# A gated linear recurrence on one core: dense scores in chunks of 128 tokens with three states each way, in place of scores for halves with one state each way

## The chip, the core and the metric

The kernel runs on one core of one Trainium2 chip. The metric is the device time of one execution in microseconds; three runs of the kernel before gave a median of 1075.76 us (1075.6 to 1076.09). Engines are named as in the profile: PE is TensorE's matmul, PEld its weight load, DVE is VectorE, ACT is ScalarE, POOL is GpSimd, SP is SyncE.

## The reference

Two layers, each with three branches on 512 tokens of width 1024. The change concerns branch A alone, a gated linear recurrence that runs over the tokens forward and backward for each of four heads (key and value width 128):

```python
def step(S, xs):
    qc, kc, vc, lfc = xs
    b = jnp.cumsum(lfc, axis=2)
    diff = b[:, :, :, None, :] - b[:, :, None, :, :]
    decay = jnp.exp(jnp.where(tri[None, None, :, :, None], diff, -jnp.inf))
    scores = jnp.einsum('bhtd,bhtsd,bhsd->bhts', qc, decay, kc)
    o = jnp.einsum('bhts,bhsv->bhtv', scores, vc) + jnp.einsum('bhtd,bhdv->bhtv', qc * jnp.exp(b), S)
    b_end = b[:, :, -1, :]
    S_new = jnp.exp(b_end)[..., None] * S + jnp.einsum(
        'bhsd,bhsv->bhdv', kc * jnp.exp(b_end[:, :, None, :] - b), vc)
    return S_new, o
```

The outputs of the two directions are added, normalised per head (an RMS norm over the 128 values) and multiplied by a SiLU gate. How the tokens are cut into chunks is free, since any cut gives the same sums: a pair of tokens (t, s) needs the product of q, k and of all gates between them.

## The kernel before

Most of the time goes to the projections: `t_block` (L516), `nat_part` (L469) and `parts_of_product` (L1200) run float32r matmuls of 512 or 256 columns in three passes (high parts, low parts of the activations, low parts of the weights) into `pm` PSUM tiles, of which there are three (`ps_main`). The weights come by DMA, are split by ScalarE and VectorE (L266, L267) a step ahead, and are used once.

Everything else is side work, written as Python generators. The main line calls `advance(us)` behind each half block of projections. It adds the time of that half block to a credit and, while the credit is positive, runs the next steps of the first two generators of the list `sides` in turn; a generator yields its own cost in us, or None to wait for the next call. The credit is cut to twice the half block's time, or to zero when the list is empty. `flush` runs generators to their end with no projections between. A scheduler of the compiler then orders each engine's instructions, so that the order in the trace can differ from the one written. Side work puts its PSUM results into `ps` tiles, of which there are five (`ps_side`).

Branch A is `gla(h, ...)`, one generator for each head. Heads run in pairs: `together` takes one step of both heads at a time, so a visit of the side work to PE holds both heads' instructions. There are two pairs in each of two layers, four in all; the second pair of a layer runs beside the branch projections `merge` and, at its end, beside `gate`.

Inside `gla` the scores of one head are built by levels m = 1, 2, 4, ..., 128. At level m a block of m tokens is paired with its neighbour block of m tokens (k of the one, q of the other, in either direction): `compact` (L925) does the levels up to 8 in 32x32 pieces, L950 the levels 16 and 32, L959 the level 64, and L974 the level 128, which pairs the two chunks of 128 tokens in each half of 256. After a level, q (`qd`, both directions) and k (`kd`) are multiplied by the gates of the neighbour block (L983, two products of 128x512 a level), and the block gates `ff` are multiplied in pairs (L986). So after level 128 q and k carry the decay to the border of their half.

The scores lie in `pm`, 128 partitions by four chunks by 256 columns, a tile of the pool `m4` (nineteen buffers of 4 KB a partition): the first copy (L963) writes the 128x128 diagonal blocks, copied predicates (L966) put the small levels into them, and L975 writes the blocks of level 128. Then, one step each: `kt`, four transposes of k (L998) copied to `kts` by L1000; the states `st`, four matmuls (L1005), two for each half of 256 tokens, copied to `sts` by L1009: one state goes from the first half to the second (forward), and one from the second to the first (backward); and the outputs `po`, for each chunk two products with `pm` (L1015) and one of q with the other half's state (L1022). `kts`, `sts`, `q`, `ksum`, `kx` (L914), the value tile `vC` of the attention and several others are tiles of the pool `t2`, seven buffers of 2 KB a partition. The normalisation follows (L1024, L1026, `rstd` at L320 to L331, L1031), then four transposes (L1036) and the product with the gate (L1037).

Of the kernel before, what the change touches and what calls it, by code (L numbers as in the profile page):

```python
# [12 lines left out]
F32 = mybir.dt.float32  # L14
# [7 lines left out]
P = 128  # L22
# [169 lines left out]
def build(nc, tc, cp, wp, sb, pp, dp, x, wpk, brow, gainb, pvec, wsp, trig, amask, imask, out):  # L192
# [397 lines left out]
    for l in range(L):  # L590
# [304 lines left out]
        def gla(h, q, ff, kd, z):  # L895
# [8 lines left out]
            pm = m4((P, 4, 256))  # L904
# [25 lines left out]
            def diag_dst(off, n):  # L930
                return custom(pm, off, ([512, 2], [384, 2], [1, n]))

# [6 lines left out]
            while m < 256:  # L939
# [16 lines left out]
                elif m == 64:  # L956
# [6 lines left out]
                    S.copy(diag_dst(0, P), dg.rearrange("p (a b) t -> p a b t", a=2))  # L963
                    for qu in range(4):
                        pr = slice(32 * qu, 32 * qu + 32)
                        V.copy_predicated(  # L966
                            diag_dst(32 * qu, 32)[pr],
                            im[pr, 4, :].unsqueeze(1).unsqueeze(1).broadcast_to((32, 2, 2, 32)),
                            pc[pr].rearrange("p (a b) t -> p a b t", a=2),
                        )  # L970
                else:
                    l128 = ps_side((P, 4, P))
                    for c in range(4):
                        E.matmul(l128[:, c, :], k_op(P * c, m), q_op(P * (c ^ 1), m), start=True, stop=True)  # L974
                    S.copy(  # L975
                        custom(pm, 128, ([512, 2], [128, 2], [1, P])), l128.rearrange("p (a b) t -> p a b t", a=2)
                    )
# [6 lines left out]
                if m < 128:  # L984
                    ffn = sb.tile([P, 2, ng], F32, name=nm("f2"), tag=f"f2_{h % 2}_{lvl % 2}", bufs=1)
                    V.tensor_tensor(ffn, fv[:, :, :, 0], fv[:, :, :, 1], ALU.mult)  # L986
                    ff = ffn
# [8 lines left out]
            kt = ps_side((P, 4, P))  # L996
            for c in range(4):
                E.transpose(kt[:, c, :], k_op(P * c, m), ident)  # L998
            kts = t2((P, 4, P))
            S.copy(kts, kt)  # L1000
            yield None
            st = ps_side((P, 2, P))
            for hf in range(2):
                for c in range(2):
                    E.matmul(  # L1005
                        st[:, hf, :], kts[:, 2 * hf + c, :], vA[hf][:, c, h * P : (h + 1) * P], start=c == 0, stop=c == 1
                    )
# [531 lines left out]
```

## Time and profile before

| | |
|---|---|
| median of three runs | 1075.76 us |
| the profiled execution | 1076.32 us |
| its span in the profile | 1074.6 us |
| PE busy | 1063.3 us (99%) |
| PEld busy | 900.7 us (84%) |
| DVE busy | 822.7 us (77%) |
| ACT busy | 491.7 us (46%) |
| POOL busy | 106.9 us (10%) |
| TensorE clock granted | full in all 40 slices |

A busy time counts each engine's instructions from their start to their end. For matmuls the end is modelled and lies behind the start of the next one, so durations of matmuls can't be added up; starts can be compared. A group of instructions is named by its line, engine and operation, then by the tiles that it writes and reads (`ps` and `pm` are PSUM tiles, `m` stands for `m4`, `t` for `t2`, `sm` for small columns). In a row of a group the count stands behind x, then busy us and the mean ns of one, then the idle time of that engine just before and what ended it.

### The profile page before, as it was taken

The page shows a single profiled execution, that of the slowest core. Times are in us where ns is not written, and L with a number is a line of the kernel's source. Part 1 is how long each engine was busy: PE and PEld are TensorE (multiplying, and loading weights), DVE is VectorE, ACT ScalarE, POOL GpSimd, SP SyncE. Part 2 cuts the span into 40 slices and gives each one's busy share as a digit, 9 for nine tenths or more (in the row PEclk, how much of TensorE's full clock was granted, in tenths as well). Part 3 has the DMA queues.
Part 4 walks back from the last instruction along what each step waited for, and adds up shares of the span by engine and source line. Part 5 has one row for each costly group of instructions (what it writes and reads, how often), then busy time and mean ns, then how long its engine had stood idle before and what let it go on. Part 6 is the DMA issues. An engine that isn't in the chain of part 4 may idle for free.

```text
span 1074.6 us, 18675 instructions
## 1 busy us (share of the span) xinstructions
PE 1063.3 (99%) x7480; PEld 900.7 (84%) x7480; DVE 822.7 (77%) x1553; ACT 491.7 (46%) x749; POOL 106.9 (10%) x150
## 2 busy tenths in 40 slices
PE   9999999999999999999999999999999999999998
PEld 8888877878788898988778888777877888999886
DVE  6974799897965975578887578998697759675885
ACT  5344665353523553545433366554444246445442
POOL 0220111000000000001112201100000001010020
PEclk9999999999999999999999999999999999999999
DMA  8673454153333464664958445434414235566665
GB/s 309 175 213 110 160 177 150 61 207 106 113 118 88 90 196 119 157 230 103 294 162 235 123 145 190 157 119 129 149 58 136 101 59 113 181 138 170 207 169 141
DMA packets 49736, 162.74 MB, mean 151 GB/s; under 512 B 5745, under 2 KB 10353, under 8 KB 49649
## 3 DMA queue, kind: packets, MB, share of 16 engines
q1 hardware_dynamic: 28656, 100.20, 28.4%
q0 software_dynamic: 19264, 57.16, 21.5%
q10 hardware_dynamic: 1728, 4.20, 1.0%
q8 instruction: 59, 0.97, 0.4%
q14 instruction: 29, 0.23, 0.1%
HBM read 139.51 MB, written 22.02 MB: 150 GB/s over the span
## 4 chain that ended last, share of the span: by engine, by line
PE 91%; DVE 5%; ACT 1%; issue 1%; DMA 1%; POOL 0%; SPq 0%; POOLq 0%; ACTq 0%; DVEq 0%
PE pm L516 48%; PE pm L469 12%; PE ps L1200 10%; PE pm L1200 9%; PE pm L504 2%; PE ps L830 2%; PE ps L925 1%; DMA wr<-in_wpk 1%; PE ps L1015 1%; PE ps L780 1%; PE ps L781 1%; DVE wl L267 1%; PE ps L974 1%; PE ps L1005 1%; PE ps L1080 1%
## 5 line engine op out<-in xcount | busy, mean ns | idle before, releaser
L266 ACT CAST wh<-wr 128x1024 fp32r<-128x1024 f32 x160 | 167.0, 1051 | 226.2 <-PE pm L516 101.9
L267 DVE TENSOR_TENSOR wl<-wr,wh 128x1024 fp32r<-128x1024 f32 x160 | 193.6, 1221 | 70.7 <-PE pm L516 42.3
L516 PE MATMUL pm<-hth,wh 128*128 128x512 f32 x576 | 230.1, 399 | 0.0
L516 PE MATMUL pm<-htl,wh 128*128 128x512 f32 x576 | 225.3, 391 | 0.0
L516 PE MATMUL pm<-hth,wl 128*128 128x512 f32 x576 | 225.0, 391 | 0.0
L516 PEld LDWEIGHTS pm<-hth,wh 128*128 128x128 f32 x576 | 108.3, 188 | 24.0 <-issue 2.9
L516 PEld LDWEIGHTS pm<-hth,wl 128*128 128x128 f32 x576 | 108.2, 188 | 23.0 <-DVE wl L267 0.2
L516 PEld LDWEIGHTS pm<-htl,wh 128*128 128x128 f32 x576 | 108.3, 188 | 21.6 <-issue 1.3
L516 PE MATMUL pm<-m,wh 128*128 128x512 f32 x256 | 90.0, 392 | 0.2 <-ACT m L1150 0.2
L983 DVE TENSOR_TENSOR m<-m,f 128x512 f32<-128x512 f32 x112 | 73.7, 688 | 5.5 <-PE ps L950 3.5
L469 PE MATMUL pm<-wh,hth 128*128 128x512 f32 x192 | 74.6, 398 | 0.7 <-ACT hth L266 0.6
L469 PE MATMUL pm<-wh,htl 128*128 128x512 f32 x192 | 73.5, 392 | 0.2 <-DVE htl L267 0.2
L469 PE MATMUL pm<-wl,hth 128*128 128x512 f32 x192 | 73.2, 392 | 0.0
L267 DVE TENSOR_TENSOR wl<-hold,wh 128x1024 fp32r<-128x1024 f32 x36 | 43.7, 1222 | 20.2 <-PE pm L1200 15.1
L266 ACT CAST wh<-hold 128x1024 fp32r<-128x1024 f32 x36 | 37.7, 1047 | 43.1 <-PE pm L516 19.6
L516 PEld LDWEIGHTS pm<-m,wh 128*128 128x128 f32 x256 | 47.8, 188 | 9.7 <-ACT m L1150 0.4
L516 PE MATMUL pm<-t,wl 128*128 128x512 f32 x128 | 50.3, 393 | 0.0
L516 PE MATMUL pm<-t,wh 128*128 128x512 f32 x128 | 50.0, 391 | 0.0
L469 PEld LDWEIGHTS pm<-wh,hth 128*128 128x128 f32 x192 | 36.0, 188 | 10.3 <-ACT hth L266 1.4
L469 PEld LDWEIGHTS pm<-wh,htl 128*128 128x128 f32 x192 | 36.1, 188 | 7.6 <-DVE htl L267 0.5
L469 PEld LDWEIGHTS pm<-wl,hth 128*128 128x128 f32 x192 | 36.1, 188 | 7.5
L266 ACT CAST m<-m 128x512 fp32r<-128x512 f32 (+1 forms) x30 | 24.4, 821 | 38.4 <-DVE m L1321 22.1
(258 smaller groups left out, 2248.1 us busy)
## 6 DMA issues: line engine op xcount, KB each, us to landing
wr<-in_wpk SPq DMA_DIRECT2D x160, 512.0 KB, 4.2
pd<-m POOLq DMA_DIRECT2D x20, 512.0 KB, 3.8
m<-pd POOLq DMA_DIRECT2D x20, 512.0 KB, 5.2
hold<-in_wpk POOLq DMA_DIRECT2D x18, 512.0 KB, 5.5
hold<-in_wpk SPq DMA_DIRECT2D x12, 512.0 KB, 4.4
wr<-in_wpk POOLq DMA_DIRECT2D x12, 512.0 KB, 7.2
m<-in_x SPq DMA_DIRECT2D x8, 512.0 KB, 7.7
m<-xd POOLq DMA_DIRECT2D x16, 256.0 KB, 7.0
```

Source lines behind the costliest of these rows:

```text
L266: order(S.copy(hi_dst, src))
L267: order(eng.tensor_tensor(lo_dst, src, hi_dst.bitcast(F32), ALU.subtract))
L469: E.matmul(po, a, b[:, o : o + 512], start=first and n == 0, stop=last and n == len(passes) - 1)
L504: E.matmul(po[:, k, :], a, b[:, o : o + 256], start=n == 0, stop=n == 23)
L516: E.matmul(po, s, m, start=n == 0, stop=n == 3 * nk - 1)
L780: E.matmul(sp[:, :nk], qt[qb][:, h, :], ktt[0][:, g, k0 * P : k1 * P], start=True, stop=False)
L781: E.matmul(sp[:, :nk], qt[qb][:, h, :], ktt[1][:, g, k0 * P : k1 * P], start=False, stop=True)
L830: E.matmul(po[64 * g : 64 * g + 64], vC[:, k0 + kb, 64 * g : 64 * g + 64], pt[:, :, 128 * g : 128 * g + 128], start=kb == 0, stop=kb == le ...
L925: E.matmul(cb[p0 : p0 + 32, slot, j // 4, :], kk(32 * j), qq(32 * j), start=True, stop=True, tile_position=(0, p0),)
L974: E.matmul(l128[:, c, :], k_op(P * c, m), q_op(P * (c ^ 1), m), start=True, stop=True)
L983: V.tensor_tensor(v, v, custom(ff, of, ([sd, 2], [2, ng], [0, m])), ALU.mult)
L1200: E.matmul(banks[g][:, r, :], a, b, start=not onto and (r, kt, n) == (0, 0, 0), stop=kt == 3 and n == 2, skip_group_check=onto is not None ...
```

## The change

The levels end at m = 64, so `pm` holds only the four 128x128 diagonal blocks, without gaps, and becomes a tile of `t2`. The level 128 goes, with its matmuls, its copy and its two products on q and k, and with one step of the generator. The part between chunks is done by states at the chunk borders instead: for each direction three chunks of k are transposed and give three states of one chunk each; a scaled addition on VectorE (the state of the chunk before, times the gate of the chunk, plus the chunk's own state) makes running states out of them, two in each direction one behind the other. An output chunk takes one product with its diagonal scores, one with the forward state where there is a chunk before it, and one with the backward state where there is one behind it. `kts` and `sts` exist once for each direction.

```diff
--- before.py
+++ after.py
@@ -1,3 +1,4 @@
+
 
 
 
@@ -901,7 +902,7 @@
             V.tensor_tensor(qd, ff, q.unsqueeze(1).broadcast_to((P, 2, T)), ALU.mult)
             cb = ps_side((P, 4, 4, 32))
             pc = sb.tile([P, 4, 32], F32, name=nm("pc"), tag="pc", bufs=2)
-            pm = m4((P, 4, 256))
+            pm = t2((P, 4, P))
 
             def q_op(t0, m):
                 if m < 32:
@@ -927,16 +928,13 @@
                         start=True, stop=True, tile_position=(0, p0),
                     )
 
-            def diag_dst(off, n):
-                return custom(pm, off, ([512, 2], [384, 2], [1, n]))
-
             m, lvl, nb = 1, 0, T
             kx = k_mix(m)
             yield 2.6
             yield None
             compact(0, lambda t: ksum[:, t : t + 32], lambda t: q[:, t : t + 32])
             V.tensor_copy(pc, cb[:, 0])
-            while m < 256:
+            while m < P:
                 if m <= 8:
                     slot = (lvl + 1) % 4
                     compact(slot, lambda t: kx[:, t : t + 32], lambda t: q_op(t, m))
@@ -953,38 +951,28 @@
                             q_op(32 * jq, m),
                             start=True, stop=True, tile_position=(0, p0),
                         )
-                elif m == 64:
+                else:
                     for j in range(8):
                         p0, f0 = 64 * (j % 2), 64 * ((j ^ 1) % 2)
                         E.matmul(
                             dg[p0 : p0 + 64, j // 2, f0 : f0 + 64], k_op(64 * j, m), q_op(64 * (j ^ 1), m),
                             start=True, stop=True, tile_position=(0, p0),
                         )
-                    S.copy(diag_dst(0, P), dg.rearrange("p (a b) t -> p a b t", a=2))
+                    S.copy(pm, dg)
                     for qu in range(4):
                         pr = slice(32 * qu, 32 * qu + 32)
                         V.copy_predicated(
-                            diag_dst(32 * qu, 32)[pr],
-                            im[pr, 4, :].unsqueeze(1).unsqueeze(1).broadcast_to((32, 2, 2, 32)),
-                            pc[pr].rearrange("p (a b) t -> p a b t", a=2),
+                            pm[pr, :, pr], im[pr, 4, :].unsqueeze(1).broadcast_to((32, 4, 32)), pc[pr]
                         )
-                else:
-                    l128 = ps_side((P, 4, P))
-                    for c in range(4):
-                        E.matmul(l128[:, c, :], k_op(P * c, m), q_op(P * (c ^ 1), m), start=True, stop=True)
-                    S.copy(
-                        custom(pm, 128, ([512, 2], [128, 2], [1, P])), l128.rearrange("p (a b) t -> p a b t", a=2)
-                    )
 
                 ng = nb // 2
                 fv = ff.rearrange("p s (g b) -> p s g b", b=2)
                 for t, of, sd in ((qd, 1, nb - 1), (kd, nb + 1, -nb - 1)):
                     v = custom(t, 0, ([T + m, 2], [2 * m, ng], [1, m]))
                     V.tensor_tensor(v, v, custom(ff, of, ([sd, 2], [2, ng], [0, m])), ALU.mult)
-                if m < 128:
-                    ffn = sb.tile([P, 2, ng], F32, name=nm("f2"), tag=f"f2_{h % 2}_{lvl % 2}", bufs=1)
-                    V.tensor_tensor(ffn, fv[:, :, :, 0], fv[:, :, :, 1], ALU.mult)
-                    ff = ffn
+                ffn = sb.tile([P, 2, ng], F32, name=nm("f2"), tag=f"f2_{h % 2}_{lvl % 2}", bufs=1)
+                V.tensor_tensor(ffn, fv[:, :, :, 0], fv[:, :, :, 1], ALU.mult)
+                ff = ffn
                 m *= 2
                 nb //= 2
                 lvl += 1
@@ -993,33 +981,39 @@
                 yield 2.6
                 yield None
 
-            kt = ps_side((P, 4, P))
-            for c in range(4):
-                E.transpose(kt[:, c, :], k_op(P * c, m), ident)
-            kts = t2((P, 4, P))
-            S.copy(kts, kt)
+
+            def v_of(c):
+                return vA[c // 2][:, c % 2, h * P : (h + 1) * P]
+
+            kts = []
+            for d in range(2):
+                kt = ps_side((P, 3, P))
+                for c in range(3):
+                    E.transpose(kt[:, c, :], kd[:, d, P * (c + d) : P * (c + d + 1)], ident)
+                kts.append(t2((P, 4, P)))
+                S.copy(kts[d][:, 0:3], kt)
             yield None
-            st = ps_side((P, 2, P))
-            for hf in range(2):
-                for c in range(2):
-                    E.matmul(
-                        st[:, hf, :], kts[:, 2 * hf + c, :], vA[hf][:, c, h * P : (h + 1) * P], start=c == 0, stop=c == 1
-                    )
-            sts = t2((P, 2, P))
-            S.copy(sts, st)
+            sts = []
+            for d in range(2):
+                st = ps_side((P, 3, P))
+                for c in range(3):
+                    E.matmul(st[:, c, :], kts[d][:, c, :], v_of(c + d), start=True, stop=True)
+                s3 = t2((P, 4, P))
+                order = (2, 1, 0) if d else (0, 1, 2)
+                S.copy(s3[:, order[0]], st[:, order[0]])
+                for a, b in zip(order, order[1:]):
+                    c = b + d
+                    c = max(a, b)
+                    V.scalar_tensor_tensor(s3[:, b], s3[:, a], ff[:, 1 - d, c : c + 1], st[:, b], ALU.mult, ALU.add)
+                sts.append(s3)
             yield None
             po = ps_side((P, 4, P))
             for t in range(4):
-                hf = t // 2
-                for c in range(2):
-                    E.matmul(
-                        po[:, t, :],
-                        pm[:, 2 * hf + c, (t % 2) * P : (t % 2 + 1) * P],
-                        vA[hf][:, c, h * P : (h + 1) * P],
-                        start=c == 0,
-                        stop=False,
-                    )
-                E.matmul(po[:, t, :], q_op(P * t, m), sts[:, 1 - hf, :], start=False, stop=True)
+                E.matmul(po[:, t, :], pm[:, t, :], v_of(t), start=True, stop=False)
+                if t > 0:
+                    E.matmul(po[:, t, :], qd[:, 1, P * t : P * t + P], sts[0][:, t - 1, :], start=False, stop=t == 3)
+                if t < 3:
+                    E.matmul(po[:, t, :], qd[:, 0, P * t : P * t + P], sts[1][:, t, :], start=False, stop=True)
             y = t2((P, 4, P))
             S.activation(y, po, AF.Square)
             ss = small(4)
```

## Rows read from the trace of the kernel before

**Rows 1.** page, part 1: span; busy us, share and instructions of each engine
```profile
span 1074.6 us, 18675 instructions
PE 1063.3 (99%) x7480; PEld 900.7 (84%) x7480; DVE 822.7 (77%) x1553; ACT 491.7 (46%) x749; POOL 106.9 (10%) x150
```

**Rows 2.** page, part 4: the chain that ended last, by engine
```profile
PE 91%; DVE 5%; ACT 1%; issue 1%; DMA 1%; POOL 0%; SPq 0%; POOLq 0%; ACTq 0%; DVEq 0%
```

**Rows 3.** waits of PE: waiter <- releaser: us in total, times, longest
```profile
PE ps L1036 <- DVE t L1031: 1.5, 2, 0.8
PE ps L1036 <- DVE sm L330: 1.0, 2, 0.6
```

**Rows 4.** PE in order of time, level 128: start us, us, line, count
```profile
327.50 0.39 PE L516 MATMUL pm<-hth,wl 128*128 128x512 f32 x1
327.73 1.95 PE L974 MATMUL ps<-m,m 128*128 128x128 f32 x16
329.43 0.48 PE L516 MATMUL pm<-hth,wh 128*128 128x512 f32 x1
329.75 0.40 PE L516 MATMUL pm<-htl,wh 128*128 128x512 f32 x1
```

**Rows 5.** the same: transposes, states, and outputs with what follows them
```profile
337.70 1.03 PE L998 MATMUL ps<-ident,m 128*128 128x128 f32 x8
338.49 0.48 PE L516 MATMUL pm<-hth,wh 128*128 128x512 f32 x1
...
341.31 1.95 PE L1005 MATMUL ps<-m,t 128*128 128x128 f32 x16
343.01 0.71 PE L516 MATMUL pm<-m,wh 128*128 128x512 f32 x2
...
345.82 0.60 PE L1015 MATMUL ps<-m,m 128*128 128x128 f32 x4
...
351.10 0.48 PE L516 MATMUL pm<-hth,wh 128*128 128x512 f32 x1
```

**Rows 6.** groups by form, PE: shapes, count; busy us, mean ns; idle before
```profile
L1015 PE MATMUL ps<-m,m 128*128 128x128 f32 x128 | 19.5, 275 | 0.0
L974 PE MATMUL ps<-m,m 128*128 128x128 f32 x64 | 7.8, 275 | 0.0
L998 PE MATMUL ps<-ident,m 128*128 128x128 f32 x32 | 4.1, 272 | 0.0
```

**Rows 7.** groups by form, VectorE and ScalarE
```profile
L983 DVE TENSOR_TENSOR m<-m,f 128x512 f32<-128x512 f32 x112 | 73.7, 688 | 5.5 <-PE ps L950 3.5 <-PE ps L959 1.0 <-ACT t L914 0.8
L1069 DVE SCALAR_TENSOR_TENSOR br<-ps,pvc,br 128x128 f32<-128x128 f32 x8 | 2.6, 331 | 0.0
L975 ACT COPY m<-ps 128x512 f32<-128x512 f32 x8 | 4.6, 585 | 5.9 <-PE ps L974 5.9
L1000 ACT COPY t<-ps 128x512 f32<-128x512 f32 x8 | 4.3, 590 | 2.3 <-PE ps L998 2.3
L1009 ACT COPY t<-ps 128x256 f32<-128x256 f32 x8 | 3.0, 370 | 8.3 <-PE ps L1005 8.3
```

**Rows 8.** PE in order of time at the last transposes; idle time and releaser bracketed
```profile
365.11 0.40 PE L1200 MATMUL pm<-m,wh 128*128 128x256 f32 x2
365.88 0.63 PE L1036 MATMUL ps<-ident,t 128*128 128x128 f32 x4 [0.37 <-DVE sm L330]
367.26 0.63 PE L1036 MATMUL ps<-ident,t 128*128 128x128 f32 x4 [0.75 <-DVE t L1031]
367.65 0.36 PE L1200 MATMUL ps<-hth,wh 128*128 128x256 f32 x1
```

**Rows 9.** waits of ScalarE
```profile
ACT t L914 <- PE ps L1036: 3.6, 2, 1.8
```

**Rows 10.** groups by form, weight loads of level 128
```profile
L974 PEld LDWEIGHTS ps<-m,m 128*128 128x128 f32 x64 | 7.8, 192 | 0.3
```

## The prediction

> **What bounds the kernel now.** I read the shares of the engines first: TensorE (PE) is busy for 1063.3 of 1074.6 us, VectorE (DVE) for 77% and ScalarE (ACT) for 46% [rows 1]. A busy PE need not be a bounding one, so the chain that ended last came next: 91% of it runs over PE [rows 2]. Third, the list of what PE waited for. Its longest entries are 1.5 and 1.0 us in the whole span, both ahead of the last transposes of the recurrence (L1036) [rows 3]. So PE sets the time almost everywhere, and the recurrence, though it is "side work" put between the blocks of the projections, is paid for in full: a PE instruction taken out of it shortens the span as long as nothing makes PE wait instead.
>
> The price of one PE instruction is not its duration in the group list (275 ns, whose end is modelled and overlaps the next one [rows 6]) but the spacing of the starts. I took it from the order in time. At the level m = 128 of the second pair of heads in layer 0, sixteen instructions start at 327.73 and the next projection matmul starts at 329.43: 1.70 us. That first matmul behind them then takes 0.32 us to the next start (329.43 to 329.75) instead of 0.23 (327.50 to 327.73), so the visit costs 1.70 + 0.09 = 1.79 us, 0.112 us for each instruction [rows 4]. The same way eight transposes cost 0.79 + 0.09 = 0.88 (0.110 each), sixteen instructions of the states 1.70 + 0.09 = 1.79, and 48 of the outputs 5.28 + 0.09 = 5.37 (0.112 each) [rows 5]. Visits of this kind cost their instructions and hardly any entry fee; each occurs four times (two pairs of heads in each of two layers), with the same gaps.
>
> **The change part by part.** The counts show that a float32 matmul of 128 columns stands as two instructions and a transpose as one: four matmuls by eight heads give x64 at L974, four transposes by eight give x32 at L998, and eight products with the scores give x128 at L1015 [rows 6]. For each pair of heads, on PE:
> - The level m = 128 goes: 2 x 4 matmuls, 16 instructions, -1.79 us.
> - Transposes of k: from 2 x 4 to 2 x 6 (three chunks each way), +4 x 0.110 = +0.44.
> - States: from 2 x 4 matmuls to 2 x 6, +8 instructions x 0.112 = +0.90.
> - Outputs: from 2 x 12 matmuls (eight with scores, four with states) to 2 x 10 (four, and three each way), -8 x 0.112 = -0.90.
>
> Sum -1.35 us a pair, four pairs, -5.4 us. All of it lies on PE, which has no cover to lose.
>
> The other engines. VectorE loses two products of 128x512 a head, 2 x 0.688, and gains four scaled additions of 128x128 out of PSUM; the nearest row is L1069, the same operation on the same shape, 0.331 [rows 7]. That is -1.376 + 1.324, nothing. ScalarE loses copies of 0.585, 0.590 and 0.370 a head; from 512 to 256 columns a copy falls by 0.220, so 384 columns are estimated at 0.48 and 128 at 0.26, two of each, 1.48 against 1.545, nothing again [rows 7]. The copy into `pm` and the four predicated copies keep their element counts: nothing. No DMA is issued, removed or moved, and no queue of SP or POOL is passed. The removed round held one `yield 2.6` a head.
>
> What is new is a chain. Before, the outputs needed only one copy of 256 columns behind the states. Now each direction needs a copy (0.26) and two dependent additions (0.331 each), about 0.92 us; two directions of two heads put 8 x 0.331 = 2.65 us on VectorE between the states and the first output that needs them. The cover is the twelve projection matmuls between the two visits, 343.01 to 345.82, 2.8 us, and the states' own visit (now 24 x 0.112 = 2.7 us), in which the first chains already run [rows 5]. So the first head's chains are covered twice, the second head's by 2.8 against 0.92 plus whatever VectorE has queued ahead; behind a late output PE's in-order queue holds the projections. The trace of before has no such wait; the nearest row is L1036, where VectorE comes late with a similar small chain and PE idles 0.37 and 0.75 us [rows 8], 2.5 us over two visits [rows 3], 1.25 a visit. I bound the new wait by 0 and 2.5 us a pair (one such wait for each head), and take 0: it is nearest to the present outputs, which follow their copies without idle time [rows 5]. A gain here has no source, since there was no wait.
>
> The L1036 wait itself (2.5 us in the two second pairs) I keep. Walking `advance` and `step` with the costs written in the code, the first pair ends one round earlier, the side list then runs empty, its credit is cut to zero, and the second pair starts a round of credit later; its last three rounds fall behind the same projection blocks as before. Its bounds are 0 and twice itself, so -2.5 to +2.5.
>
> Buffers: `pm` moves from the nineteen `m4` to the seven `t2`, and a head has two `kts` and two `sts` where it had one of each. The pool is already full at times: the copy of L914 waits for L1036 for 3.6 us in two waits, although it reads only k, so what it waits for is a buffer [rows 9]. In a first pair, with `vC` and the next head's `q` still alive, two `pm` and four states make eight, so the second head's last state waits for the first head's outputs and PE may see one more chain of 0.92: 0 to 0.9 us in two pairs, 0 to 1.8 in all. I take 0, because PE has projection blocks to put there, and an eviction held up by the pool stops PE only when all three `pm` PSUM banks are full. [...]
>
> The sum: -5.4 us. The profiled execution took 1076.32 us, 1.72 more than its span of 1074.6, so 1070.9 for it; it lies 0.56 above the median of 1075.76, and from the median the forecast is 1070.4 us. A measurement of this kernel can tell about 0.2% (2.15 us) from no change.
>
> **The rivals.**
> - *The wait at L1036 goes too.* If the earlier end of the chains lets the last normalisation run ahead of the sums of the next stage on VectorE, 2.5 us more are gained: 1067.9. For it: VectorE has 2.8 us a pair less in the removed round. Against it: the credits above put the tail where it was.
> - *Half of it comes back.* One wait of 1.25 us a pair at the outputs, 4 x 1.25 = 5.0: -0.4, 1075.4, within 0.2%.
> - *Slower: PE waits for the states' chains.* The place is the first output with a state, in all four pairs; both heads wait 1.25, 2.5 a pair, 10 us in all: +4.6, 1080.3. It decides from (5.4 + 2.15) / 4 = 1.9 us a pair. For it: two dependent additions and a copy more, a full `t2` pool, and VectorE at 77%. Against it: 2.8 us of projections between the visits, and more to be put there.
> - *Weight loads set the pace.* If each instruction cost what its weight load lasts, 0.192 us [rows 10], and the transposes' the 0.11 above, then 16 x 0.192 - 0.44 = 2.63 a pair would go, 10.5 in all: 1065.2. Against it: the sixteen start 0.106 us apart [rows 4], so loads overlap each other. [...]
>
> **How the numbers follow.** Forecast with up to 2.5 us either way (1068.3 to 1073), 0.62; L1036 gone, 0.12; weight loads, 0.04; half back, 0.12; slower, 0.10. Faster by over 0.2% is 0.62 + 0.12 + 0.04 = 0.78, within 0.12, slower 0.10. The range takes in the first, second and fourth case: 1067.0, a little under 1067.9, to 1076.0, a little over 1075.4; it leaves out 0.14.
>
> **What would show it.** PE's instructions fall by 6 a head (-8, +2, +4, -4), 48 in all, from 7480 to 7432. Transposes stand as x48 and states as x96; no 128x512 copy follows a level 128. The spacing in the new visits is 0.11 us. The four additions a head are near 0.33 us, 32 in all. PE's wait list shows no entry of over 1 us at an output line; if it shows the additions as releaser there, the third or second rival holds. The span falls by 5.4 us. I am wrong if the count falls as said and the span does not: then PE's idle time or its gaps have grown, and the line behind the gap names the step.

## The result, and the profile after

The changed kernel takes 1067.13 us (median of four runs, 1066.56 to 1067.98), beside 1075.70 for the kernel before on the same chip (1075.6 to 1076.09): a ratio of 0.992, 95% interval 0.9903 to 0.9937, or 8.6 us less. The forecast was 1070.4, 5.4 us less. The sign was right, but 3.2 us more went than the instructions account for, and the time lies only 0.1 us above the lower end of the range (1067.0). The profiled execution took 1067.56 us with a span of 1065.8; the span fell by 8.8 us, and the ledger below is made against that.

The page of the changed kernel, parts 1 and 4 (span, busy us of each engine, the chain that ended last), which answers to [rows 1, 2]:

```profile
span 1065.8 us, 18593 instructions
PE 1057.0 (99%) x7432; PEld 894.3 (84%) x7432; DVE 822.6 (77%) x1569; ACT 490.3 (46%) x757; POOL 106.7 (10%) x150
...
PE 94%; DVE 3%; DMA 1%; ACT 1%; issue 0%; SPq 0%; ACTq 0%; POOLq 0%; DVEq 0%
```

PE has the 48 instructions fewer that were forecast, VectorE's and ScalarE's busy time has hardly moved (822.7 and 491.7 before), and PE's share of the chain that ended last rises from 91% to 94%. The share points to where the surplus lies: in time that PE had spent waiting.

The longest wait of PE at a line of the recurrence in the changed kernel (waiter, releaser, us in total, times, longest), which answers to [rows 3]:

```profile
PE ps L1016 <- DVE t L1007: 0.9, 1, 0.9
```

Two things are to be read here. The line of the last transposes (L1036 before, L1030 now), with 1.5 and 1.0 us the longest entries of the recurrence, is not in the list any more. And the two new ones are small: one output product waits once for a scaled addition, and one group of state products once, 0.3 us, for a copy of k (in the rows at 236.39 below).

The new work, groups by form (line, engine, tiles, shapes, count; busy us, mean ns; idle before), which answers to [rows 6, 7]:

```profile
L992 PE MATMUL ps<-ident,m 128*128 128x128 f32 x48 | 5.9, 272 | 0.0
L1000 PE MATMUL ps<-m,t 128*128 128x128 f32 x96 | 11.6, 276 | 0.3 <-ACT t L994 0.3
L1007 DVE SCALAR_TENSOR_TENSOR t<-t,f,ps 128x128 f32<-128x128 f32 x32 | 9.5, 345 | 5.9 <-ACT t L1003 5.7
L994 ACT COPY t<-ps 128x384 f32<-128x384 f32 x16 | 6.7, 488 | 5.8 <-PE ps L992 3.5 <-PE ps L1000 2.3
L1003 ACT COPY t<-ps 128x128 f32<-128x128 f32 x16 | 4.2, 268 | 11.3 <-PE ps L1000 6.1 <-PE ps L1016 5.2
```

PE in order of time at the new transposes and states of one pair (start us, us, line, count, idle time before), which answers to [rows 5]:

```profile
229.83 1.47 PE L992 MATMUL ps<-ident,m 128*128 128x128 f32 x12
231.06 0.48 PE L517 MATMUL pm<-hth,wh 128*128 128x512 f32 x1
...
233.91 2.17 PE L1000 MATMUL ps<-m,t 128*128 128x128 f32 x18
236.39 0.94 PE L1000 MATMUL ps<-m,t 128*128 128x128 f32 x6 [0.31 <-ACT t L994]
```

Twelve transposes take 229.83 to 231.06, 1.23 us, plus the 0.09 by which the projection matmul behind them is longer: 1.32, or 0.110 each, as forecast. The second head's last six state instructions start at 236.39 instead of 233.91 + 18 x 0.112 = 235.93, so this visit holds a gap of 0.5 us.

The last transposes of the second pair in layer 0, the place of [rows 8], in the changed kernel:

```profile
362.30 0.66 PE L1030 MATMUL ps<-ident,t 128*128 128x128 f32 x4
...
363.48 0.66 PE L1030 MATMUL ps<-ident,t 128*128 128x128 f32 x4
```

Neither visit has idle time in brackets now, and five projection matmuls stand between the two heads.

Where the 8.8 us of the span went, summed from the starts on PE (a gap is the distance between two starts less the usual one of that shape):

| | us |
|---|---|
| 48 instructions fewer, as forecast | -5.4 |
| gaps at the last transposes of the two second pairs (before 0.53, 0.91, 0.78 and 0.92; after 0.3 in all) | -2.8 |
| gaps where one layer ends (see g1_before: perhaps not in every execution) | -1.2 |
| first steps of the second pairs (L925 behind `pc`, 0.42 twice) | -0.8 |
| one gap near 887 us | -0.4 |
| the states' gap at 236.39 | +0.5 |
| the outputs' wait at 345.92 (below, with the runs on the chain) | +1.0 |
| sum | -9.1 |

0.3 us of it stay without a place.

### The profile page after: what moved, and what is told of

It reads as the page before. It is cut to its first block, busy times and chain, and to the rows that moved or that the text cites. A ratio compares the mean times of both kernels' runs of the same rounds, so it can differ in the third digit from the quotient of the medians.

```text
span 1065.8 us, 18593 instructions
## 1 busy us (share of the span) xinstructions
PE 1057.0 (99%) x7432; PEld 894.3 (84%) x7432; DVE 822.6 (77%) x1569; ACT 490.3 (46%) x757; POOL 106.7 (10%) x150
## 4 chain that ended last, share of the span: by engine, by line
PE 94%; DVE 3%; DMA 1%; ACT 1%; issue 0%; SPq 0%; ACTq 0%; POOLq 0%; DVEq 0%
PE pm L517 48%; PE pm L470 12%; PE ps L1194 11%; PE pm L1194 11%; PE pm L505 2%; PE ps L831 2%; PE ps L926 1%; PE ps L781 1%; PE ps L782 1%; PE ps L1000 1%; PE ps L1012 1%; PE ps L1074 1%; DMA wr<-in_wpk 1%; DVE wl L268 1%; DMA hold<-in_wpk 1%; PE ps L948 1%
## 5 line engine op out<-in xcount | busy, mean ns | idle before, releaser
L267 ACT CAST wh<-wr 128x1024 fp32r<-128x1024 f32 x160 | 167.0, 1051 | 242.1 <-PE pm L517 125.0
L972 DVE TENSOR_TENSOR m<-m,f 128x512 f32<-128x512 f32 x96 | 63.6, 688 | 4.0 <-PE ps L948 3.9
L267 ACT CAST wh<-hold 128x1024 fp32r<-128x1024 f32 x36 | 37.8, 1049 | 45.4 <-PE pm L517 18.1
L267 ACT CAST m<-m 128x512 fp32r<-128x512 f32 (+1 forms) x30 | 24.2, 820 | 38.4 <-DVE m L1315 22.0
```

Source lines behind the costliest of these rows:

```text
L267: order(S.copy(hi_dst, src))
L972: V.tensor_tensor(v, v, custom(ff, of, ([sd, 2], [2, ng], [0, m])), ALU.mult)
```

## The experiments

### Why the last transposes no longer wait

Three theories stood. **A**: the removed round of the generator, which brings everything behind it forward. **B**: VectorE's lighter load, the reason that the prediction's first rival gave. **C**: buffers. `pm` left the pool of nineteen 4 KB tiles, so in a pair two tiles of `m4` more are free for the sums of the next stage and their splits, which are `m4` tiles too.

**B, by the kernel before without the two products of level 128.** Label e2_no_products, an edit of the kernel before:

```diff
-                for t, of, sd in ((qd, 1, nb - 1), (kd, nb + 1, -nb - 1)):
+                for t, of, sd in ((qd, 1, nb - 1), (kd, nb + 1, -nb - 1)) if m < 128 else ():
```

> The kernel before, without the two products of level 128 on q and k (VectorE, 128x512 each, two a head): this leaves out part of the computation. PE's instructions and the rounds stay. Theory B, VectorE's load makes the last transposes late: 16 x 0.69 = 11 us less on VectorE, PE's wait at L1036 shrinks from 2.5 us to under 0.5, and the time is about 1073 us. Theory A, the round does it: 1075.7 us, wait as before.

Measured: 1075.18 us, ratio 0.9999 (0.999 to 1.0007). The waits of PE in it:

```profile
PE ps L1036 <- DVE t L1031: 1.5, 2, 0.8
...
PE ps L1036 <- DVE sm L330: 1.0, 2, 0.6
```

They are those of [rows 3] to the digit. Taking 11 us of busy VectorE time (16 products of 0.688) out of this chain gains nothing, so B falls.

**A, by the change with the removed round put back, empty.** Label e1_round_kept, an edit of the changed kernel:

```diff
                 yield 2.6
                 yield None
 
+            yield 2.6
+            yield None
 
             def v_of(c):
```

> The changed kernel with the removed round put back as an empty one (the yield of 2.6 and the None stay, no work in them), so that the steps of the recurrence fall behind the same projection blocks as before the change. It computes the same. PE's instructions stay 7432. Theory A, the gain beyond the count of PE's instructions comes from the removed round, which changes what VectorE has queued ahead of the last normalisation: the wait of PE at the last transposes (L1036 before) comes back and the time is about 1070 us, 2.5 to 3 us above the changed kernel. Theory B, it comes from the work taken off VectorE: about 1067 us, as the changed kernel, and no such wait.

Measured: 1068.31 us (1067.8 to 1068.54), ratio 0.9935 (0.9923 to 0.9948). The last transposes do not appear among PE's waits, so the round is not what took that wait away: A falls for it. What does come back, with 0.5 us in the list of waits, is the one at the first steps of the second pairs:

```profile
PE ps L926 <- DVE pc L936: 0.5, 2, 0.2
```

By the medians the round is worth 1.2 us, by the spans of the two profiles 0.6. The two intervals overlap, so that the round has a worth rests on the row more than on the time.

**C, by the same kernel with `pm` in the pool `m4` again.** Label f2_round_m4, the edit of e1_round_kept and

```diff
-            pm = t2((P, 4, P))
+            pm = m4((P, 4, P))
```

> The changed kernel with the removed round kept as an empty one and the scores tile pm back in the pool of 4 KB buffers: rounds and buffers as before the change, only the instructions of the change differ. It computes the same. Theory C, the gain beyond the count came from buffers (pm no longer holds two of the nineteen while the sums of the next stage want them): the wait of some 2.5 us at the last transposes is back and the time is what the count alone gives, 1075.4 - 5.4 = 1070.0 us. Theory D, it came from the new instructions themselves: no such wait, 1067 to 1068.3 us. If the 4 KB pool is what cost 13.6 us in the run with pm in it, whatever the round: about 1080.

Measured: 1070.82 us (1070.62 to 1071.26), ratio 0.9956 (0.9943 to 0.9968). The waits of PE and, behind them, one of VectorE:

```profile
PE ps L1032 <- DVE t L1027: 2.7, 4, 0.8
...
DVE m L268 <- PE ps L1014: 2.8, 2, 1.7
```

With the instructions of the change, but the rounds and the pools of before, the wait at the last transposes is back (2.7 us in four), and the gain over the kernel before is 4.7 us, near the 5.4 of the instruction count. From here to e1_round_kept only the pool of `pm` differs, and that is 2.5 us.

**C, by one buffer fewer.** Label g3_18, an edit of the changed kernel:

```diff
-N_M4, N_T2, N_PM, N_PS = 19, 7, 3, 5
+N_M4, N_T2, N_PM, N_PS = 18, 7, 3, 5
```

> The changed kernel with eighteen 4 KB buffers in place of nineteen. It computes the same. Theory C, the 4 KB buffers that pm no longer holds are what took the wait at the last transposes away: one buffer less brings part of the waits back, there or at the outputs, 1068.5 to 1071 us. If these buffers are in no shortage: 1067.1.

Measured: 1068.24 us (1068.13 to 1068.5), ratio 0.9936 (0.9922 to 0.995), 1.1 us over the change. The wait of PE in question:

```profile
PE ps L1030 <- DVE t L1025: 1.2, 2, 0.7
```

Nothing but the number of buffers differs from the changed kernel, and part of the wait is back; in PE's order the last transposes of layer 0 stand behind 1320 and 1322 projection matmuls, as in the kernel before (1322), where the change has 1303 and 1308. C holds. The other direction, the kernel before with more 4 KB buffers, was not tried.

How two free buffers end a wait of PE 15 us later can be followed on VectorE, in layer 0. The kernel before, VectorE in order of time:

```profile
348.55 1.23 DVE L267 TENSOR_TENSOR m<-m,m 128x1024 fp32r<-128x1024 f32 x1 [3.18 <-PE ps L1015]
...
350.82 0.68 DVE L1026 TENSOR_REDUCE sm<-t 128x4 f32<-128x512 f32 x1
...
359.03 1.22 DVE L267 TENSOR_TENSOR m<-m,m 128x1024 fp32r<-128x1024 f32 x1
...
360.24 0.68 DVE L1026 TENSOR_REDUCE sm<-t 128x4 f32<-128x512 f32 x1
...
366.43 0.69 DVE L1031 TENSOR_TENSOR t<-ps,sm 128x512 f32<-128x512 f32 x1
```

The first row is the split of a sum for the next stage. It reads nothing of the outputs (L1015), yet it waits 3.18 us for them: what it waits for is the tile that they free, `pm`. The next stage's sums and splits, the last of them at 359.03, then stand between the first head's reduction for the norm (350.82) and the second head's (360.24), and the second head's scaling (L1031) ends only at 367.1, which is the wait of [rows 8]. The changed kernel, the same engine:

```profile
354.46 0.68 DVE L1020 TENSOR_REDUCE sm<-t 128x4 f32<-128x512 f32 x1
355.05 1.22 DVE L268 TENSOR_TENSOR m<-m,m 128x1024 fp32r<-128x1024 f32 x1
...
362.74 0.69 DVE L1025 TENSOR_TENSOR t<-ps,sm 128x512 f32<-128x512 f32 x1
```

The second head's reduction comes 5.8 us earlier, now ahead of a split, and the scaling 3.7 (PE's order leads by about 1 us there already). In the kernels in which the wait is back the old order is back too, in layer 0. VectorE in f2_round_m4 there:

```profile
356.45 1.23 DVE L268 TENSOR_TENSOR m<-m,m 128x1024 fp32r<-128x1024 f32 x1
...
357.67 0.68 DVE L1022 TENSOR_REDUCE sm<-t 128x4 f32<-128x512 f32 x1
```

In g3_18 the split starts at 356.39 and the reduction at 357.60. That the buffers are the cause is shown by f2_round_m4 and g3_18; that it goes by this order on VectorE is read from these four traces, which agree in layer 0, and was not tested by itself. In layer 1 the order does not tell the kernels apart: in the change the second head's reduction stands behind a split there too (882.66 behind 880.79) and PE does not wait, in f2_round_m4 it stands ahead of one (885.07 before 885.94) and PE waits. What makes the normalisation late in layer 1 stays open.

### The two parts don't add: the round without the buffers

Label e4_pm_m4, the changed kernel (round removed) with `pm` in `m4`:

```diff
-            pm = t2((P, 4, P))
+            pm = m4((P, 4, P))
```

> The changed kernel with the scores tile pm taken from the pool of nineteen 4 KB buffers, as before the change, in place of the pool of seven 2 KB buffers. It computes the same. If the fuller pool costs nothing on PE: 1067.1 us within 0.7. If the second head's late states in the first pairs cost PE 0.9 us each: about 1065.3, and the second head's outputs then follow the first head's without projection matmuls between. If the gain beyond the count came from the freed large buffers (loads and splits that start earlier): 1069 to 1070.

Measured: 1080.72 us (1079.01 to 1081.08), ratio 1.0047 (1.0034 to 1.0059): 13.6 us over the change and slower than the kernel before. No theory had this. The loss lies in the second pair of layer 1. PE in order of time there, then the copies into `pm` on ScalarE, in the changed kernel and in this one, and below them this kernel's windows (stretch, its length, PE busy, granted clock as a share of full, DMA share, GB/s):

```profile
871.57 1.36 PE L1000 MATMUL ps<-m,t 128*128 128x128 f32 x6 [2.11 <-DVE t L1007]
...
882.15 0.77 PE L1012 MATMUL ps<-m,m 128*128 128x128 f32 x2 [3.29 <-DVE m L964]
882.72 0.63 PE L1016 MATMUL ps<-t,m 128*128 128x128 f32 x2
883.14 0.63 PE L1012 MATMUL ps<-m,m 128*128 128x128 f32 x2
...
888.07 0.46 PE L1012 MATMUL ps<-m,m 128*128 128x128 f32 x2 [1.84 <-DVE m L964]
```

```profile
853.91 1.06 ACT L961 COPY t<-ps 128x512 f32<-128x512 f32 x2
```

```profile
879.78 0.59 ACT L961 COPY m<-ps 128x512 f32<-128x512 f32 x1
...
886.08 0.59 ACT L961 COPY m<-ps 128x512 f32<-128x512 f32 x1 [5.71 <-PE ps L1012]
```

```profile
868.00:880.00 12.00, 8.75 (x37) 0.86 0.28 44
880.00:900.00 20.00, 16.00 (x95) 0.83 0.32 74
```

The changed kernel copies both heads' level 64 into `pm` together, at 853.91. Here the first copy comes at 879.78 and the second at 886.08, after 5.71 us of waiting for the first head's outputs, which it does not read: what they free is a 4 KB tile (the pool of `pm` is all that differs from the changed kernel). The copied predicates (L964) follow these copies, and the outputs follow the predicates: PE waits 3.29 us ahead of the first head's outputs and 1.84 ahead of the second's. The wait of 2.11 us at the second head's states is another one: it ends with scaled additions of states, whose results these matmuls do not read. By the program they free a `ps` tile, and two of the five still held the scores of level 64 that had not been copied; this is read from the trace and not tested. PE's three waits are 2.1 + 3.3 + 1.8 = 7.2 us, and behind each the granted clock was lower for a while: 0.66 of full from 871 to 876 behind the first, 0.50 for about 3 us behind each of the others (last section). By the windows that is 0.14 of 12 us and 0.17 of 20 us, 5.1 us. Together 12.3, of some 13 us by which this stretch of PE's order grew. So removing the round costs 9.9 us where `pm` lies in `m4` (f2_round_m4 to e4_pm_m4) and gains about 1.2 where it lies in `t2` (e1_round_kept to the change). The buffer move is what makes the removed round safe.

### The price of an instruction on PE

Label e3_level_twice, the kernel before with the matmuls of level 128 written twice:

```diff
-                    for c in range(4):
+                    for c in (0, 1, 2, 3) * 2:
                         E.matmul(l128[:, c, :], k_op(P * c, m), q_op(P * (c ^ 1), m), start=True, stop=True)
```

> The kernel before with the matmuls of level 128 issued twice into the same PSUM tile, 16 instructions more on PE in each of the four pairs. It computes the same. If an instruction costs its spacing of 0.112 us on the time: 4 x 16 x 0.112 = 7.2 us more, 1082.9 us. If it costs its weight load of 0.192 us: 12.3 us more, 1088.0. If the recurrence were hidden beside other work: 1075.7.

Measured: 1081.52 us (1081.36 to 1083.69), ratio 1.0064 (1.0051 to 1.0078), 6.1 us more. The visit of [rows 4], PE in order of time, with 32 instructions in place of 16:

```profile
329.40 3.73 PE L974 MATMUL ps<-m,m 128*128 128x128 f32 x32
332.89 0.48 PE L516 MATMUL pm<-hth,wh 128*128 128x512 f32 x1
```

3.49 + 0.09 = 3.58 us, 0.112 each, and 1.79 more than [rows 4] in each of the four visits: 7.2 us. By the spans of the two profiles 5.2 came, since the gaps at the end of the layer, 1.2 us in the ledger and 1.4 with the longer instructions behind them, are missing in this one (more on them at g1_before). Had each instruction cost what its weight load lasts [rows 10], 16 x 0.192 x 4 = 12.3 us would have come. The measured spacing decides here, and it is 0.112, not 0.192.

### The new chain between states and outputs

What the change pays there, PE in order of time in the changed kernel:

```profile
344.66 0.38 PE L1012 MATMUL ps<-m,t 128*128 128x128 f32 x2
345.92 0.49 PE L1016 MATMUL ps<-t,m 128*128 128x128 f32 x2 [0.87 <-DVE t L1007]
```

This is the second pair of layer 0: the first output has its product with scores, and its product with the backward state, the last link of that chain, comes 1.0 us late (345.92 instead of 344.66 + 2 x 0.112 = 344.88). The other three pairs have no such wait. What made it late is the term that the prediction left open, "whatever VectorE has queued ahead": seven of the eight additions start only at 344.74, behind the split of a weight.

```profile
343.61 1.22 DVE L268 TENSOR_TENSOR wl<-hold,wh 128x1024 fp32r<-128x1024 f32 x1
344.74 2.02 DVE L1007 SCALAR_TENSOR_TENSOR t<-t,f,ps 128x128 f32<-128x128 f32 x7
```

**The chain taken away.** Label e6_no_additions, an edit of the changed kernel:

```diff
-                S.copy(s3[:, order[0]], st[:, order[0]])
-                for a, b in zip(order, order[1:]):
-                    c = b + d
-                    c = max(a, b)
-                    V.scalar_tensor_tensor(s3[:, b], s3[:, a], ff[:, 1 - d, c : c + 1], st[:, b], ALU.mult, ALU.add)
+                S.copy(s3[:, 0:3], st)
```

> The changed kernel without the additions between the states: each direction's three states are copied at once, each chunk's own, so this leaves out part of the computation. PE's instructions stay. 8 x 0.27 us a pair less on VectorE, and no dependent chain between states and outputs. If the chain costs PE only the wait seen in layer 0: about 1 us less, 1066.1. If it costs more through VectorE's queue, as the slower rival had it: 1064 or less. If nothing: 1067.1.

Measured: 1066.67 us (1066.49 to 1066.94), ratio 0.9917 (0.9903 to 0.993). The output's wait is gone from the list, and the time is 0.5 us under the change, which is less than these runs tell apart. All 32 additions together cost at most about 1 us.

**The chain three times as long.** Label e7_additions_thrice:

```diff
-                    V.scalar_tensor_tensor(s3[:, b], s3[:, a], ff[:, 1 - d, c : c + 1], st[:, b], ALU.mult, ALU.add)
+                    for _ in range(3):
+                        V.scalar_tensor_tensor(s3[:, b], s3[:, a], ff[:, 1 - d, c : c + 1], st[:, b], ALU.mult, ALU.add)
```

> The changed kernel with each addition of states issued three times (the same result written thrice): 16 more on VectorE in each pair, a chain of 0.26 + 6 x 0.27 = 1.9 us for each direction and some 6.5 us of VectorE between states and outputs, against 2.8 + 2.7 us of PE's work there. It computes the same. If projection blocks are put in front of the late outputs: under 1 us more, 1068. If PE waits for the chains as the slower rival had it: 1 to 3 us a pair, 1071 to 1079.

Measured: 1071.53 us (1070.46 to 1072.88), ratio 0.9963 (0.995 to 0.9975), 4.4 over the change. PE in order of time, and a window behind it (columns as in e4_pm_m4):

```profile
347.04 0.46 PE L1013 MATMUL ps<-m,t 128*128 128x128 f32 x2 [1.92 <-DVE t L1008]
```

```profile
347.80:351.10 3.30, 3.30 (x15) 0.50 0.68 133
```

Projection blocks are put in front of the second head's outputs (17 to 36 matmuls later in PE's order than in the change), as the prediction said, and yet PE waits, above all in one pair of four. It waits there at the second head's first product with scores, which reads no state; by the program the additions can hold it up only by the `ps` tiles that they still read, which was not tested. Behind the wait this profiled execution, 1.4 us over the median, has a granted clock of 0.50. So PE can be made to wait for the chains, as the slower rival had it, though mostly not at the place that it named; the chain as it is lies well short of the point from which this decides.

**The products with scores first.** Label e5_scores_first, the same instructions in another order, so that each output needs its states only after all four products with scores:

```diff
             for t in range(4):
-                E.matmul(po[:, t, :], pm[:, t, :], v_of(t), start=True, stop=False)
+                E.matmul(po[:, t, :], pm[:, t, :], v_of(t), start=t == 0, stop=False, skip_group_check=True)
+            for t in range(4):
                 if t > 0:
...
```

(The marks of the accumulation group in the lines that follow are set to match.)

> The changed kernel with the four products with pm ahead of all products with states in each head's outputs (one accumulation group in the bank). It computes the same, with the same instructions. The first product with a state then comes 3 x 2 x 0.112 = 0.7 us later. If PE's wait of 0.9 us there in layer 0 is for the additions: it shrinks to 0.2 and the time is 1066.4. If nothing waits there in most executions: 1067.1.

Measured: 1066.11 us (1066.06 to 1066.28), ratio 0.9912 (0.9898 to 0.9925). PE in order of time:

```profile
344.03 1.05 PE L1012 MATMUL ps<-m,t 128*128 128x128 f32 x8
344.92 0.39 PE L1017 MATMUL ps<-t,m 128*128 128x128 f32 x2
```

Eight instructions with scores stand in place of the idle time, and the wait is gone. This is the fastest version, 1.0 us under the change and 9.4 under the kernel before. Its slowest run lies under the change's fastest, though on another chip, and the intervals of the two ratios overlap. Taking the additions away (e6_no_additions, the same chip) gained only 0.5, so about half of this 1.0 us is not shown to be the wait.

### What else was tried

**More 2 KB buffers at the cost of one of 4 KB.** Label g2_scores_first_18_9, an edit of e5_scores_first:

```diff
-N_M4, N_T2, N_PM, N_PS = 19, 7, 3, 5
+N_M4, N_T2, N_PM, N_PS = 18, 9, 3, 5
```

> The kernel with the products with pm first, with eighteen 4 KB buffers and nine 2 KB buffers (the same space). It computes the same. If the 2 KB pool makes the second head's outputs late in the first pairs and this costs PE: the projection matmuls between the two heads' outputs are gone and the time is 1065.5. If the 4 KB buffers are the scarcer ones: 1067 to 1070, with waits at the last transposes or the outputs of the second pairs.

Measured: 1067.71 us (1067.4 to 1067.84), ratio 0.993 (0.9917 to 0.9943), 1.6 more than e5_scores_first. In the list of PE's waits the last transposes are back:

```profile
PE ps L1031 <- DVE t L1026: 1.2, 2, 0.7
```

In the first pairs both heads' outputs stand in one visit, where the change has three projection matmuls between them, but so they do in e5_scores_first with its seven buffers. What the two more buffers do shows on ScalarE, at the second head's last copies of states in the first pair (e5_scores_first, then this run):

```profile
240.35 0.27 ACT L1003 COPY t<-ps 128x128 f32<-128x128 f32 x1 [3.31 <-PE ps L1012]
```

```profile
235.63 0.59 ACT L1003 COPY t<-ps 128x128 f32<-128x128 f32 x3
```

With seven buffers the copy waits for outputs that it does not read (4.23 us in the change, 4.24 in g3_18, which has seven as well), with nine it does not: the pool `t2` was full there, as the prediction worked out. The fourth copy of k (L994) tells the same: at 235.86 in the change and 235.23 in e5_scores_first, over 4 us behind the third, and in one row with the other three from 230.08 on with nine buffers. For PE this brings nothing that shows, while one 4 KB buffer fewer brings a wait back: the 4 KB tiles are the scarce ones.

**The kernel before, once more.** Label g1_before, without an edit, for the gaps at the end of the layer:

> The kernel before once more, for a second profile of it. If the two gaps of 0.5 and 0.7 us at the border of the two layers, which the first profile has and no other run shows, belong to that execution alone: they are gone here, and the span is about 1.2 us shorter, near 1073.4 us. If they belong to the kernel: 1074.6 again. The waits at the last transposes (2.5 us) stand in both cases. Time 1075.5, ratio 1.000.

Measured: 1075.53 us, ratio 1.0004 (0.9995 to 1.0013), span 1074.9. The rows of the first profile of before, PE in order of time:

```profile
521.02 0.50 PE L1200 MATMUL ps<-wh,sh 128*128 128x512 f32 x1 [0.37 <-ACT wh L266]
...
522.28 0.50 PE L1200 MATMUL ps<-wl,sh 128*128 128x512 f32 x1 [0.53 <-DVE wl L267]
```

In this second profile the gaps are there again, at 521.08 and 522.34, 0.36 and 0.69 us over the usual distance of 0.23 (before: 0.53 and 0.69); in the changed kernel's profile and in those of the edited ones they are not, but for 0.23 us at 521.22 in e2_no_products. So they are no accident of one execution. But both profiled executions of before lie above the medians of their kernel (1076.32 beside 1075.76, 1076.74 beside 1075.53), by 0.6 and 1.2 us beside gaps of 1.2 and 1.05, so whether all its executions have them is not known. PE waits there for the parts of a weight. The first product of `wh` with `sh` starts at 513.69 before; where it starts at 511.62 (the change) and at 517.13 (e3_level_twice) the wait is not there, but e2_no_products, where that product starts at 513.74, has only those 0.23 us too; why it falls just there stays open.

## Why the prediction was right in part

The ladder from kernel to kernel, medians:

| kernel | what differs from the one above | us | step |
|---|---|---|---|
| before | | 1075.5 | |
| f2_round_m4 | the new instructions alone | 1070.8 | -4.7 |
| e1_round_kept | `pm` in `t2` | 1068.3 | -2.5 |
| the change | the round removed | 1067.1 | -1.2 |
| e5_scores_first | products with scores first | 1066.1 | -1.0 |

The runs come from several chips, on which the kernel before took 1075.4 to 1075.7; by the ratios to it the steps are -4.7, -2.3, -1.6 and -0.9. The first is clear of noise, and so is the second by the runs themselves, which do not overlap; the sizes of the last two are not.

**Right: what bounds the kernel, and the count.** PE's instructions fell by 48, transposes stand as x48, states as x96. The spacing of 0.112 was confirmed by doubling a visit (e3_level_twice: 1.79 us more), and at that spacing the weight loads, 0.192 each [rows 10], do not set the pace, so the rival of 1065.2 falls. The first rung, which holds little more than the count and the new chain, is 4.7 against 5.4.

**Right: VectorE and ScalarE neutral.** The additions took 0.345 (0.331 forecast), the copies of 384 and of 128 columns 0.488 and 0.268 (0.48 and 0.26).

**Nearly right: the new chain at nothing.** It made one wait of 0.87 us, inside the bounds of 0 and 2.5 a pair. The cover named, twelve projection matmuls, was enough for the first outputs in three pairs of four. The prediction's own sign, "if it shows the additions as releaser there, the third or second rival holds", came up with this wait although neither rival holds: the sign lacked a size.

**Right: the `t2` side of the buffers.** The pool was full in the first pairs (g2_scores_first_18_9), and already at the fourth copy of k, earlier than the prediction had it. PE lost nothing by it but the 0.5 us at 236.39, whose releaser is that copy: it stood behind a cast (L267, at 234.91) that had waited 3.32 us for its DMA. In e5_scores_first, where the cast ended 0.6 us earlier, PE has no gap there.

**Wrong: "The L1036 wait itself (2.5 us in the two second pairs) I keep."** The walk through the credits was right in its own terms: in both kernels k is transposed behind 1212 projection matmuls of layer 0, the states follow behind 1224 and the outputs behind 1236. But from equal places of the outputs it does not follow that the wait stays, for what made the last normalisation late was not where the outputs stood. The step that failed is one of pricing a move from one side only: `pm` was put into `t2` and costed there, and what the two tiles that it leaves in `m4` are worth was not asked. The trace of before had it, in the waits of VectorE:

```profile
DVE m L267 <- PE ps L1022: 3.8, 1, 3.8
...
DVE m L267 <- PE ps L1015: 3.2, 1, 3.2
```

These are two splits of the next stage's sums waiting for outputs that they do not read, one in each second pair: a full pool, 7 us in all, and [rows 9] had shown the same sign on the other pool. The range had the case, since the bound of -2.5 was set by the whole wait; the stretch given to the forecast itself, 1068.3 to 1073, had not (from 1070.4, a bound of -2.5 would have put its lower end at 1067.9). That the time stayed inside is partly luck: by the ledger, beyond this wait, some 2.4 us went by terms that the prediction did not have (the first steps, the end of the layer, the gap near 887) and 1.5 came back at the states and outputs.

**Right for the wrong reason: the first rival.** Its time, 1067.9, is 0.8 from the result, the wait at L1036 did go, and in layer 0 the last normalisation does run ahead of a split of the next stage on VectorE, as it said. But its cause, an earlier end of the chains by VectorE's lighter load, is refuted by e2_no_products (no change at all) and, for the removed round, by e1_round_kept (the wait stays away with the round back). Its weight of 0.12 came from the same one-sided view.

**Left out: the round's own worth.** The prediction let a round of credit go at no price. It gained some 1.2 us where buffers were free (0.6 by the spans, 1.6 by the ratios), mostly at the first steps of the second pairs (0.8 us in the ledger), and cost 9.9 where they were not. The 1.2 us at the end of the layer, as far as they count at all, could not have been read from the change.

**The other rivals.** Half back (1075.4) and slower (1080.3) did not come. Tripled additions brought 4.4 us, near the 5.0 that the half-back rival had put on the chain, but with one wait of 1.9 us in one pair and not one of 1.25 in each.

## What to carry to other kernels

When a tile moves from one pool to another, price both pools: list the waits of VectorE and ScalarE for instructions whose results they do not read (here 3.8 and 3.2 us on VectorE before the change, and they were waits for buffers), and ask what they delay. Price an instruction on a saturated PE by the spacing of its starts (0.112 us here), not by its duration (0.275) nor by its weight load (0.192). Two edits that are safe together need not be so apart: the same removed round gained about 1.2 us with the buffers free and cost 9.9 without.

## What the runs showed of the hardware

The stretch of the stalls in e4_pm_m4 grew by more than their length. PE stood still for 3.29 us ahead of 882.15, and in the matmuls that followed (882.72 to 885.27) a pair of instructions takes 0.43 us from start to start where it takes 0.22 elsewhere. The windows of that trace (columns as above):

```profile
882.50:885.50 3.00, 3.00 (x16) 0.50 0.36 141
...
888.90:891.80 2.90, 2.90 (x16) 0.50 0.35 68
```

The granted clock was 0.50 of full for 3 us behind that stall, then full (1.00 from 888.0 to 888.9), and 0.50 again for 2.9 us from 888.9 on, though the stall of 1.84 us had ended at 888.07. The short wait of 0.87 us ahead of 345.92 in the changed kernel left no such trace: the granted clock from 345.5 to 350 is 1.00 there; behind the 1.92 us of e7_additions_thrice it was 0.50. Beside the three waits of e4_pm_m4, 7.2 us, thus stand 5.1 us by the lower clock; what lowers it was not tested. The times of single executions agree: of e4_pm_m4 the three with a mean clock of 0.995 took 1080.7 to 1081.1 us and the two with 0.997 took 1079.0 and 1079.6; of e7_additions_thrice the two with 0.998 took 1072.2 and 1072.9 and the three with 1.000 took 1070.5 to 1071.5.
